# Split decays for the triangular sums, an earlier split of the gate factor, and no context modulation in the last layer

## The chip, the cores and the metric

The kernel runs on 1 core of one Trainium2 chip. The metric is the device time of one execution, in microseconds (us). A profiled execution gives its span (from the first to the last instruction on the core) and the trace from which all rows below are read.

## The reference

Two layers of a backbone work on 256 latent tokens and 256 context tokens of width 1024. Each layer has a modulated RMS norm, one input projection, three token mixers side by side (differential attention, chunked gated linear attention "GLA", neighbourhood attention), a gated merge with an output projection, then a second modulated norm and a squared-ReLU MLP. All is float32. What matters here:

```python
# modulation: six vectors of 1024 per layer, for the latent stream and for the context stream
mod = jax.nn.silu(c) @ w_mod[l] + b_mod[l]
mod_c = jax.nn.silu(c_ctx) @ w_mod[l] + b_mod[l]
sh1, sc1, g1, sh2, sc2, g2 = split(mod, 6);  sh1c, sc1c, g1c, sh2c, sc2c, g2c = split(mod_c, 6)
# the log decays of GLA, for the forward and the backward direction
z = ga[..., i * 16:(i + 1) * 16] @ a2[i] + ab[i]
log_a = log_sigmoid(z) / 16
cum = jnp.cumsum(log_a, within chunks of 64)
qe = q * exp(cum);  ke = k * exp(-cum);  kd = k * exp(cum_last - cum)
# the last layer returns the latent stream alone: there the context stream needs sh1c and sc1c only
if need_ctx:
    ctx = ctx + g1c * m_ctx
    ctx = ctx + g2c * sqrelu_mlp(rms_norm(ctx, norm2_g[l]) * (1.0 + sc2c) + sh2c, w_ff1[l], w_ff2[l])
```

## The kernel before

**Matrix products.** A product of two float32 operands is one matmul call, which the compiler turns into two matrix instructions (names as `pss<-la,tri` in the trace). Most products avoid it: both operands are split into a rounded half of type float32r ("high") and the remainder ("low"), and three calls (high by high, high by low, low by high) of one instruction each replace it. `split` does this for a tile: `copy` rounds it on ScalarE or VectorE (`act_first` picks the one that the planner expects to be done first), and VectorE subtracts. Weights come as pieces of 128x1024: a DMA on SP's queue into one of five `raw` buffers, a ScalarE copy (`wh<-raw`), a VectorE subtraction (`wl<-raw,wh`); `take()` hands the next piece to a product.

**Order.** Nothing is scheduled by the compiler: `drive` runs generators ("tasks") that emit instructions, and each engine, and each DMA queue, executes its instructions in the order in which they were emitted. A task yields a function that returns when its next step can start. `drive` takes the first task (in a fixed list: norms, attention, modulation, and last the stream of weight products) whose time has come by the planner's clock of TensorE, or else the one that comes first, and moves that clock there. The clock and the readiness of tiles come from constants of the kernel: a DMA takes `DMA_PER_BYTE` (2.9 us per MiB) after the last one, plus `LATENCY["DMA"]` = 2.0 us; an instruction takes `FIXED` + elements x `PER`. These constants decide the order only.

Two rules of lateness matter. A weight piece is split ahead of its use only while the planned ScalarE and VectorE are no further ahead of TensorE than `SPLIT_LATE` says, by how many pieces ahead it is:

```python
SPLIT_LATE = (INF, 1.5, 0.5, 0.0, 0.0, 0.0)     # us, index: pieces ahead of the one in use
if max(now["ACT"], now["DVE"]) > now["PE"] + SPLIT_LATE[min(n - st["cur"], 5)]: return False
```

A modulation product (`mods_task`; VectorE multiplies a 128x512 weight tile `wm` by the broadcast vector `cb` and sums along the row, once for the latent vector into `dump`, once for the context vector in place) is let in while VectorE is planned at most 1.0 us ahead of TensorE.

**The GLA gate.** The job `ga` starts behind the q/k products (`qk`) and ahead of the v products (`gv`). It issues three DMAs on SP's queue (`sb`, and the two `gl` tiles `ab` and `a2`), takes its weight piece, runs 24 matmuls (`psg<-h,wh` and `psg<-h,wl`, 512 columns), and splits their result into `gat`; then it splits the factor `a2` into `a2s`, which the trace calls `a`. `gla` waits for both, then multiplies (`pss<-a,gat`, 4 matmuls) and makes the log decays `la` on VectorE and ScalarE, and `tile_steps` sums them with the triangular matrices `tri` (`pss<-la,tri`) and with `ind`. While `gla` waits, the stream goes on with `gv`.

**Neighbourhood attention** of the first layer starts (in `branches`) when the last modulation group of that layer is done.

Of the kernel before, what the change touches and what calls it, by code (L numbers as in the profile page):

```python
# [151 lines left out]
def build(nc, tc, ctx, a):  # L152
# [18 lines left out]
    def const(name, shape, dtype=F32):  # L171
        return cpool.tile(shape, dtype, name=name, tag=name)
# [25 lines left out]
    def need(*aps, ps=None, n=1, lane=None, late=1.0):  # L198

        def f():  # L200
            t = pl.ready(aps)
            if ps:
                tag = ps if ps in PS else "s"
                i = n - 1 - (PS[tag] - len(ring.get(tag, ())))
                if i >= 0:
                    t = max(t, pl.touched(ring[tag][i]))
            if lane:
                t = max(t, now[lane] - late)
            return t
        return f  # L210
# [167 lines left out]
    ones = const("ones", [P, P])  # L378
    V.memset(ones, 1.0)
    rope = const("rope", [P, 2, 2, HD])  # L380
    tri = const("tri", [P, 4, P])
    ind = const("ind", [P, P])
    msk = const("msk", [P, 2, 4, P], U8)
    cc = const("cc", [P, KT, 2])
# [5 lines left out]
    scl = [[const(f"scl{l}{n}", [P, KT, 2]) for n in range(2)] for l in range(DEPTH)]  # L390


    def mod_scale(l, n, k0, k1):

        s = scl[l][n][:, k0:k1]
        g = sa[l][:, (SA_N1 if n == 0 else SA_N2) + k0:][:, 0:k1 - k0].unsqueeze(2).to_broadcast([P, k1 - k0, 2])
        V.scalar_tensor_tensor(s, mod[l][1 + 3 * n][:, k0:k1], 1.0, g, ADD, MULT)

    def mods_task():

        for l in range(DEPTH):
            yield after("consts" if l == 0 else MOD1_AFTER)

            groups = ((2, 4, 3, 5), range(6))[l]
            acc = {g: small("macc", [P, 2, KT, 2], 6) for g in groups}
            for ih in ((0,), (1,)) if l == 0 else ((0, 1),):
                cb = {}
                th = {}
                for i in ih:
                    for s in range(2):  # L410
                        cb[i, s], th[i, s] = u("cb"), u("cbt")
                        S.dma_start(cb[i, s], a["cr"][s, i].partition_broadcast(P))
                yield need(*cb.values(), lane="ACT")
                for k, c in cb.items():
                    S.activation(th[k], c, AF.Tanh, scale=0.5)
                    V.tensor_scalar(th[k], th[k], 0.5, 0.5, MULT, ADD)
                    G.tensor_tensor(c, c, th[k], MULT)
                todo = [(g, k, i) for g in groups for k in range(KT) for i in ih]
                loaded = []

                def load():
                    if todo:
                        g, k, i = todo.pop(0)
                        loaded.append((g, k, i, buf("wm", "wm", 512, NWM)))
                        MQ.dma_start(loaded[-1][3], a["w_mod"][l, g * KT + k, i])

                for _ in range(NWM):
                    load()
                while loaded:
                    g, k, i, w = loaded.pop(0)  # L430
                    for s in range(2):
                        yield need(w, cb[i, s], lane="DVE", late=MOD_LATE[l])
                        V.scalar_tensor_tensor(u("dump") if s == 0 else w, w, 1.0, cb[i, s], MULT, MULT,
                                               accum_out=acc[g][:, i, k, s:s + 1])
                    load()
                    if k == KT - 1 and i == 1:
                        yield need(acc[g], lane="DVE")
                        m = mod[l][g]
                        V.tensor_tensor(m, acc[g][:, 0], acc[g][:, 1], ADD)
                        b = sa[l][:, SA_BMOD + g * KT:SA_BMOD + (g + 1) * KT].unsqueeze(2).to_broadcast([P, KT, 2])  # L440
                        V.tensor_tensor(m, m, b, ADD)
                        if g in (1, 4):
                            mod_scale(l, g // 4, 0, KT)
                        done.add(("mod", l, g))


# [474 lines left out]
    def gla(L, y):  # L921
# [15 lines left out]
        yield need(*lt, lane="ACT")  # L937
        for t in (2, 3, 0, 1):
            S.activation(lt[t], lt[t], AF.Ln, bias=1.0)
        for t in (2, 3, 0, 1):  # L940
            V.scalar_tensor_tensor(la[t], la[t], 0.0, lt[t], ALU.min, SUB)

        yield after((l, "gv"))
        am0 = [u("amask") for _ in range(2)]
# [7 lines left out]
        for stage in range(2):  # L952
            tl = (2, 3) if stage == 0 else (0, 1)
            outs = stage == 1 or need_ctx
            qeT, at, ds, dec = [None] * 2, [None] * 2, [None] * 2, [None] * 2

            def tile_steps(b, t):
                lat = la[t]
                yield need(lat, ps="s")
                pr = psum("s")  # L960
                for r in range(2):
                    mm(hrd(pr)[:, :, r], tri[:, 2 + r, :], hrd(lat)[:, :, r], True, True)
                kd = u("kd")
                S.activation(kd, pr, AF.Exp)
                V.tensor_tensor(hrd(kd), hrd(kd), bc(qk[t][:, 256:512]), MULT)
                yield need(lat, ps="t")
                pd = psum("t")
                for h in range(4):
                    mm(pd[:, h * P:(h + 1) * P], lat[:, h * P:(h + 1) * P], ind, True, True)
                dc = small("dec", [P, 4, 2], 4)  # L970
                S.activation(dc, pd.rearrange("p (h c r) -> p h c r", h=4, c=2)[:, :, :, 0], AF.Exp)
                dec[b] = dc
                if outs:
                    yield need(lat, ps="s")
                    pc = psum("s")
                    for r in range(2):
                        mm(hrd(pc)[:, :, r], tri[:, r, :], hrd(lat)[:, :, r], True, True)
                    qe = u("qe")
                    S.activation(qe, pc, AF.Exp)
                    ke = u("ke")  # L980
                    S.activation(ke, pc, AF.Exp, scale=-1.0)
                    V.tensor_tensor(hrd(qe), hrd(qe), bc(qk[t][:, 0:256]), MULT)
                    V.tensor_tensor(hrd(ke), hrd(ke), bc(qk[t][:, 256:512]), MULT)
                ds[b] = []
                yield need(kd, ps="s", n=2)
                px = [psum("s"), psum("s")]
                for h in range(4):
                    for c in range(2):
                        rows = slice(64 * c, 64 * c + 64)
                        PE.matmul(px[c][:, h * P:(h + 1) * P], kd[rows, h * P:(h + 1) * P],  # L990
                                  v[t][rows, h * P:(h + 1) * P], start=True, stop=True, tile_position=(64 * c, 0))
                for c in range(2):
                    ds[b].append(u("ds"))
                    copy(ds[b][c], px[c])
                if not outs:
                    return
                yield need(ke, ps="t")
                keT = u("keT")
                copy(keT, transpose_4(ke))
                yield need(qe, ps="t")  # L1000
                qT = u("qeT")
                copy(qT, transpose_4(qe), HD ** -0.5)
                qeT[b] = qT
                yield need(keT, qT, ps="s", n=2)
                px = [psum("s"), psum("s")]
                for h in range(4):
                    for r in range(2):
                        rows = slice(64 * r, 64 * r + 64)
                        PE.matmul(px[r][:, h * P:(h + 1) * P], keT[rows, h * P:(h + 1) * P],
                                  qT[rows, h * P:(h + 1) * P], start=True, stop=True, tile_position=(64 * r, 0))  # L1010
                for r in range(2):
                    V.copy_predicated(am0[r], msk[:, r].rearrange("p h c -> p (h c)"), px[r])
                am = u("am")
                V.tensor_tensor(am, am0[0], am0[1], ADD)
                at[b] = am
# [50 lines left out]
    def start(l, h):  # L1066
# [25 lines left out]
        def ga():  # L1092
# [5 lines left out]

            a2s = u("a2", dtype=F32R)[0:96]
            L["gl"] = ab, a2s  # L1100
            yield piece
            w = take()
            yield need(*w, ps="g")
# [5 lines left out]
            gat = u("gat", dtype=F32R)[0:96]  # L1109
            copy(gat, ps[0:96])  # L1110
            V.tensor_tensor(gat[32:64], ps[32:64], gat[32:64].bitcast(F32), SUB)
            copy(a2s, a2[0:96])
            V.tensor_tensor(a2s[64:96], a2[64:96], a2s[64:96].bitcast(F32), SUB)
            L["gat"] = gat

        jobs.append(((l, "ga"), None, ga))
# [380 lines left out]
    def first_norm():  # L1497
# [13 lines left out]
            return after(("m01", k))()  # L1511

        yield from norm_apply(0, 0, x0, pb, 0, NTOK, NTOK, h, [0, 1], ready)
        for dst, n in ((tri, "tri"), (ind, "ind"), (rope, "rope")):
            S.dma_start(dst, a[n])
        mskf = u("mskf")[:, :2 * P].rearrange("p (r c) -> p r c", r=2)
        S.dma_start(mskf, a["msk"].rearrange("p (r c) -> p r c", r=2))
        for r in range(2):
# [136 lines left out]
```

## Time and profile before

| | |
|---|---|
| median of 3 runs | 1530.45 us (1530.14 to 1531.07) |
| the profiled execution | 1532.37 us, span 1530.3 us |
| mean granted TensorE clock | 0.998 of full |
| TensorE matmul busy (PE) | 1501.4 us, 98% of the span |
| VectorE busy (DVE) | 1105.0 us, 72% |
| ScalarE busy (ACT) | 705.2 us, 46% |
| GpSimd busy (POOL) | 22.5 us, 1% |
| DMA moved | 216.66 MB |

All instructions carry the line of one helper (L133), so rows are told apart by tile names, written `out<-in`. Matmuls are pipelined: the duration shown is longer than the time that one adds, which is the distance between starts. An entry in brackets at the end of a timeline row is the idle time of the engine before it and what ended it. SPq is SP's queue of DMA issues.

### The profile page before, as it was taken

To read this page: it belongs to the slowest core of one execution; us is meant where nothing else is said; L and a number is where in the kernel's file an instruction comes from. 1 tells how busy PE (TensorE), PEld (TensorE's weight loads), DVE (VectorE), ACT (ScalarE), POOL (GpSimd) and SP (SyncE) were. 2 spreads that over 40 slices of the span, in tenths; PEclk is the share of its full clock that TensorE was granted. 3 is DMA by queue.
4 is the path that set the end of the run, shared out by engine and by line. 5 is a ranking of instruction groups with operands and counts; after the bars stand their busy time and mean duration, and the time that the engine had idled before them with its cause. 6 is when DMAs were issued, how large, how long until landed. Compare 5 with 4: busy or idle time off the path is not lost.

```text
span 1530.3 us, 24161 instructions
## 1 busy us (share of the span) xinstructions
PE 1501.4 (98%) x9340; PEld 1281.9 (84%) x9340; DVE 1105.0 (72%) x2360; ACT 705.2 (46%) x1236; POOL 22.5 (1%) x30
## 2 busy tenths in 40 slices
PE   7999999999999899999999999999999999999999
PEld 5788878888887788888888888788888899899999
DVE  5687886687996676697786957777876766785543
ACT  4543535543235533723324153454465565477632
POOL 0100000000000100100000000000000000000000
PEclk9999999999999999999999999999999999999999
DMA  9531321157642232365564743322224325345662
GB/s 355 198 111 63 113 81 56 56 165 227 216 135 80 87 103 91 130 199 181 174 202 150 228 139 125 118 82 97 97 83 138 131 91 186 132 162 197 206 202 75
DMA packets 77794, 216.66 MB, mean 142 GB/s; under 512 B 9073, under 2 KB 12529, under 8 KB 77681
## 3 DMA queue, kind: packets, MB, share of 16 engines
q1 hardware_dynamic: 74880, 210.28, 42.3%
q10 hardware_dynamic: 2160, 2.76, 0.6%
q0 software_dynamic: 640, 2.10, 0.4%
q8 instruction: 73, 1.20, 0.3%
q14 instruction: 41, 0.33, 0.1%
HBM read 214.05 MB, written 1.05 MB: 141 GB/s over the span
## 4 chain that ended last, share of the span: by engine, by line
PE 89%; DVE 6%; ACT 2%; DMA 2%; issue 1%; SPq 0%; ACTq 0%; DVEq 0%
PE psg L133 77%; PE pss L133 12%; DVE wl L133 1%; ACT wh L133 1%; DMA wm<-w_mod 1%; DVE hn L133 1%; DMA gl<-gl 1%; DVE h L133 1%; DVE x L133 0%; DVE nt L133 0%; DMA sa<-sa 0%; ACT e L133 0%; SPq L133 0%; DVE nr L133 0%; ACT h L133 0%
## 5 line engine op out<-in xcount | busy, mean ns | idle before, releaser
L133 DVE TENSOR_TENSOR wl<-raw,wh 128x1024 fp32r<-128x1024 f32 x290 | 353.3, 1228 | 143.2 <-ACT wh L133 142.6
L133 PE MATMUL psg<-h,wh 128*128 128x256 f32 (+1 forms) x1808 | 447.3, 338 | 1.7 <-ACT wh L133 0.7
L133 ACT ACTIVATE wh<-raw 128x1024 fp32r<-128x1024 f32 x290 | 300.4, 1052 | 179.2 <-PE psg L133 166.4
L133 PEld LDWEIGHTS psg<-h,wh 128*128 128x128 f32 x1808 | 305.7, 189 | 42.3 <-issue 6.2
L133 PE MATMUL psg<-wh,h 128*128 128x512 f32 (+1 forms) x1056 | 338.8, 395 | 0.8 <-ACT h L133 0.8
L133 PE MATMUL psg<-h,wl 128*128 128x256 f32 (+1 forms) x904 | 302.8, 335 | 0.8 <-DVE wl L133 0.8
L133 PE MATMUL psg<-act,wh 128*128 128x256 f32 (+1 forms) x1056 | 250.8, 330 | 0.0
L133 PEld LDWEIGHTS psg<-wh,h 128*128 128x128 f32 x1056 | 197.2, 188 | 48.9 <-issue 2.1
L133 PE MATMUL psg<-wl,h 128*128 128x512 f32 (+1 forms) x528 | 206.7, 392 | 0.0
L133 PEld LDWEIGHTS psg<-act,wh 128*128 128x128 f32 x1056 | 178.2, 188 | 19.1
L133 PEld LDWEIGHTS psg<-h,wl 128*128 128x128 f32 x904 | 170.9, 189 | 19.5 <-DVE wl L133 1.2
L133 PE MATMUL psg<-act,wl 128*128 128x256 f32 (+1 forms) x528 | 174.4, 330 | 0.0
L133 DVE SCALAR_TENSOR_TENSOR dump<-wm,cb 128x512 f32<-128x512 f32 x160 | 109.7, 686 | 10.8 <-DMA wm<-w_mod 10.6
L133 PEld LDWEIGHTS psg<-wl,h 128*128 128x128 f32 x528 | 99.3, 188 | 21.3
L133 DVE SCALAR_TENSOR_TENSOR wm<-wm,cb 128x512 f32<-128x512 f32 x160 | 110.3, 689 | 4.0
L133 PEld LDWEIGHTS psg<-act,wl 128*128 128x128 f32 x528 | 99.2, 188 | 10.6
L133 PE MATMUL psg<-y,wh 128*128 128x512 f32 (+1 forms) x384 | 95.8, 339 | 0.0
L133 DVE TENSOR_TENSOR act<-r,act 128x256 fp32r<-128x256 f32 (+1 forms) x65 | 35.1, 540 | 72.8 <-ACT act L133 72.8
L133 ACT ACTIVATE r<-psg 128x256 f32<-128x256 f32 (+1 forms) x63 | 30.0, 476 | 107.5 <-PE psg L133 107.3
L133 PEld LDWEIGHTS psg<-y,wh 128*128 128x128 f32 x384 | 64.7, 188 | 8.8 <-issue 1.1
L133 PE MATMUL psg<-sp,wh 128*128 128x256 f32 (+1 forms) x304 | 65.3, 311 | 1.8 <-ACT sp L133 1.4
L133 PE MATMUL psg<-y,wl 128*128 128x512 f32 (+1 forms) x192 | 64.6, 337 | 0.0
(220 smaller groups left out, 1654.1 us busy)
## 6 DMA issues: line engine op xcount, KB each, us to landing
raw<-w_ff SPq DMA_DIRECT2D x128, 512.0 KB, 4.3
wm<-w_mod SPq DMA_DIRECT2D x192, 256.0 KB, 3.8
raw<-w_tok SPq DMA_DIRECT2D x72, 512.0 KB, 3.9
raw<-w_gate SPq DMA_DIRECT2D x48, 512.0 KB, 4.0
raw<-w_br SPq DMA_DIRECT2D x24, 512.0 KB, 3.6
raw<-w_out SPq DMA_DIRECT2D x16, 512.0 KB, 3.9
tb<-natb SPq DMA_DIRECT2D x16, 192.0 KB, 3.9
x<-xc SPq DMA_DIRECT2D x8, 256.0 KB, 4.5
```

Source lines behind the costliest of these rows:

```text
L133: r = f(*args, **kw)
```

## The change

Three edits. (1) In `gla`, each of the four decay tiles `la[t]` is split into two float32r halves, and each triangular sum (`sums`) becomes two float32r calls with the matrix `tri`, which is now float32r (its values are exact there; it is loaded through a float32 tile `trif` and copied by VectorE, after `ind` and `rope` on ScalarE's DMA queue). (2) In `ga`, the split of `a2` moves ahead of the job's weight piece and products, behind a wait for `a2`. (3) In the last layer, modulation groups 2 to 5 are computed for the latent vector alone.

```diff
--- before.py
+++ after.py
@@ -378,7 +378,7 @@
     ones = const("ones", [P, P])
     V.memset(ones, 1.0)
     rope = const("rope", [P, 2, 2, HD])
-    tri = const("tri", [P, 4, P])
+    tri = const("tri", [P, 4, P], F32R)
     ind = const("ind", [P, P])
     msk = const("msk", [P, 2, 4, P], U8)
     cc = const("cc", [P, KT, 2])
@@ -390,11 +390,11 @@
     scl = [[const(f"scl{l}{n}", [P, KT, 2]) for n in range(2)] for l in range(DEPTH)]
 
 
-    def mod_scale(l, n, k0, k1):
-
-        s = scl[l][n][:, k0:k1]
-        g = sa[l][:, (SA_N1 if n == 0 else SA_N2) + k0:][:, 0:k1 - k0].unsqueeze(2).to_broadcast([P, k1 - k0, 2])
-        V.scalar_tensor_tensor(s, mod[l][1 + 3 * n][:, k0:k1], 1.0, g, ADD, MULT)
+    def mod_scale(l, n, k0, k1, ns=2):
+
+        s = scl[l][n][:, k0:k1, :ns]
+        g = sa[l][:, (SA_N1 if n == 0 else SA_N2) + k0:][:, 0:k1 - k0].unsqueeze(2).to_broadcast([P, k1 - k0, ns])
+        V.scalar_tensor_tensor(s, mod[l][1 + 3 * n][:, k0:k1, :ns], 1.0, g, ADD, MULT)
 
     def mods_task():
 
@@ -429,18 +429,21 @@
                 while loaded:
                     g, k, i, w = loaded.pop(0)
                     for s in range(2):
+                        if l == DEPTH - 1 and s == 1 and g > 1:
+                            continue
                         yield need(w, cb[i, s], lane="DVE", late=MOD_LATE[l])
                         V.scalar_tensor_tensor(u("dump") if s == 0 else w, w, 1.0, cb[i, s], MULT, MULT,
                                                accum_out=acc[g][:, i, k, s:s + 1])
                     load()
                     if k == KT - 1 and i == 1:
                         yield need(acc[g], lane="DVE")
-                        m = mod[l][g]
-                        V.tensor_tensor(m, acc[g][:, 0], acc[g][:, 1], ADD)
-                        b = sa[l][:, SA_BMOD + g * KT:SA_BMOD + (g + 1) * KT].unsqueeze(2).to_broadcast([P, KT, 2])
+                        ns = 1 if l == DEPTH - 1 and g > 1 else 2
+                        m = mod[l][g][:, :, :ns]
+                        V.tensor_tensor(m, acc[g][:, 0, :, :ns], acc[g][:, 1, :, :ns], ADD)
+                        b = sa[l][:, SA_BMOD + g * KT:SA_BMOD + (g + 1) * KT].unsqueeze(2).to_broadcast([P, KT, ns])
                         V.tensor_tensor(m, m, b, ADD)
                         if g in (1, 4):
-                            mod_scale(l, g // 4, 0, KT)
+                            mod_scale(l, g // 4, 0, KT, ns)
                         done.add(("mod", l, g))
 
 
@@ -937,8 +940,11 @@
         yield need(*lt, lane="ACT")
         for t in (2, 3, 0, 1):
             S.activation(lt[t], lt[t], AF.Ln, bias=1.0)
+        las = [None] * 4
         for t in (2, 3, 0, 1):
             V.scalar_tensor_tensor(la[t], la[t], 0.0, lt[t], ALU.min, SUB)
+        for t in (2, 3, 0, 1):
+            las[t] = split(la[t])
 
         yield after((l, "gv"))
         am0 = [u("amask") for _ in range(2)]
@@ -954,12 +960,18 @@
             outs = stage == 1 or need_ctx
             qeT, at, ds, dec = [None] * 2, [None] * 2, [None] * 2, [None] * 2
 
+            def sums(i, t):
+
+                ps = psum("s")
+                for r in range(2):
+                    for j, x in enumerate(las[t]):
+                        mm(hrd(ps)[:, :, r], tri[:, i + r, :], hrd(x)[:, :, r], j == 0, j == 1)
+                return ps
+
             def tile_steps(b, t):
                 lat = la[t]
-                yield need(lat, ps="s")
-                pr = psum("s")
-                for r in range(2):
-                    mm(hrd(pr)[:, :, r], tri[:, 2 + r, :], hrd(lat)[:, :, r], True, True)
+                yield need(*las[t], ps="s")
+                pr = sums(2, t)
                 kd = u("kd")
                 S.activation(kd, pr, AF.Exp)
                 V.tensor_tensor(hrd(kd), hrd(kd), bc(qk[t][:, 256:512]), MULT)
@@ -971,10 +983,8 @@
                 S.activation(dc, pd.rearrange("p (h c r) -> p h c r", h=4, c=2)[:, :, :, 0], AF.Exp)
                 dec[b] = dc
                 if outs:
-                    yield need(lat, ps="s")
-                    pc = psum("s")
-                    for r in range(2):
-                        mm(hrd(pc)[:, :, r], tri[:, r, :], hrd(lat)[:, :, r], True, True)
+                    yield need(*las[t], ps="s")
+                    pc = sums(0, t)
                     qe = u("qe")
                     S.activation(qe, pc, AF.Exp)
                     ke = u("ke")
@@ -1098,6 +1108,9 @@
 
             a2s = u("a2", dtype=F32R)[0:96]
             L["gl"] = ab, a2s
+            yield need(a2)
+            copy(a2s, a2[0:96])
+            V.tensor_tensor(a2s[64:96], a2[64:96], a2s[64:96].bitcast(F32), SUB)
             yield piece
             w = take()
             yield need(*w, ps="g")
@@ -1109,8 +1122,6 @@
             gat = u("gat", dtype=F32R)[0:96]
             copy(gat, ps[0:96])
             V.tensor_tensor(gat[32:64], ps[32:64], gat[32:64].bitcast(F32), SUB)
-            copy(a2s, a2[0:96])
-            V.tensor_tensor(a2s[64:96], a2[64:96], a2s[64:96].bitcast(F32), SUB)
             L["gat"] = gat
 
         jobs.append(((l, "ga"), None, ga))
@@ -1511,8 +1522,11 @@
             return after(("m01", k))()
 
         yield from norm_apply(0, 0, x0, pb, 0, NTOK, NTOK, h, [0, 1], ready)
-        for dst, n in ((tri, "tri"), (ind, "ind"), (rope, "rope")):
+        for dst, n in ((ind, "ind"), (rope, "rope")):
             S.dma_start(dst, a[n])
+        trif = u("trif").rearrange("p (r c) -> p r c", r=4)
+        S.dma_start(trif, a["tri"])
+        V.tensor_copy(tri, trif)
         mskf = u("mskf")[:, :2 * P].rearrange("p (r c) -> p r c", r=2)
         S.dma_start(mskf, a["msk"].rearrange("p (r c) -> p r c", r=2))
         for r in range(2):
```

## Rows read from the trace of the kernel before

**Rows 1.** Page: busy time, share of the span, instructions

```profile
PE 1501.4 (98%) x9340; PEld 1281.9 (84%) x9340; DVE 1105.0 (72%) x2360; ACT 705.2 (46%) x1236; POOL 22.5 (1%) x30
```

**Rows 2.** Busy time by stretches: stretch, length, engines, clock, DMA share, GB/s

```profile
840.00:870.00 30.00, 30.00 (x133) 24.62 (x132) 29.55 (x78) 5.75 (x6) 0.00 (x0) 1.00 0.76 226
```

**Rows 3.** Groups by shape: count, then busy us, mean ns, idle before

```profile
L133 DVE SCALAR_TENSOR_TENSOR dump<-wm,cb 128x512 f32<-128x512 f32 x160 | 109.7, 686 | 10.8 <-DMA wm<-w_mod 10.6
L133 DVE DVE_READ_ACCUMULATOR wm<-wm,cb 128x1 f32 x160 | 13.1, 82 | 0.0
L133 DVE TENSOR_TENSOR sp<-m,sp 128x512 fp32r<-128x512 f32 x12 | 8.3, 692 | 8.5 <-ACT sp L133 8.5
L133 DVE TENSOR_TENSOR wl<-raw,wh 128x1024 fp32r<-128x1024 f32 x290 | 353.3, 1228 | 143.2 <-ACT wh L133 142.6 <-DMA wm<-w_mod 0.3
```

**Rows 4.** Tile tri; timeline of PE from 82 us; the chain's last row

```profile
L133 PE MATMUL pss<-la,tri x56: 377/379/454, 82.2 to 1032.5; 128*128 128x256 f32 x56
...
82.18 1.02 PE L133 MATMUL pss<-la,tri 128*128 128x256 f32 x4
83.04 1.05 PE L133 MATMUL pss<-ind,la 128*128 128x128 f32 x8
...
1353.65 173.37 PE psg L133 x1454
```

**Rows 5.** Timeline of the first layer's gate (SP, PE, ACT, DVE)

```profile
53.58 0.86 SPq L133 DMA_DIRECT2D gl<-gl  x2
57.26 0.39 PE L133 MATMUL psg<-wh,h 128*128 128x512 f32 x1
60.14 0.63 ACT L133 ACTIVATE a<-gl 96x512 fp32r<-96x512 f32 x1 [2.08 <-DMA gl<-gl]
60.80 0.68 DVE L133 TENSOR_TENSOR a<-gl,a 32x512 fp32r<-32x512 f32 x1 [2.02 <-ACT a L133]
61.54 1.20 PE L133 MATMUL pss<-a,gat 96*128 96x512 f32 x4 [1.31 <-DVE a L133]
63.04 0.69 DVE L133 SCALAR_TENSOR_TENSOR dump<-wm,cb 128x512 f32<-128x512 f32 x1 [1.38 <-DMA wm<-w_mod]
```

**Rows 6.** Timeline of the last layer's gate

```profile
982.58 2.94 ACT L133 ACTIVATE wh<-raw 128x1024 fp32r<-128x1024 f32 x3
984.00 0.90 SPq L133 DMA_DIRECT2D gl<-gl  x2
987.60 0.39 PE L133 MATMUL psg<-wh,h 128*128 128x512 f32 x1
990.64 0.63 ACT L133 ACTIVATE a<-gl 96x512 fp32r<-96x512 f32 x1 [2.25 <-DMA gl<-gl]
992.04 1.20 PE L133 MATMUL pss<-a,gat 96*128 96x512 f32 x4 [1.49 <-DVE a L133]
```

**Rows 7.** Landing times: tiles gl and wm; issues from 972 to 996 us

```profile
DMA to landing us min/median/max: 5.4/6.0/6.1
...
DMA to landing us min/median/max: 2.5/3.8/7.7
...
sb<-sb SPq DMA_DIRECT2D x1, 258.0 KB, 4.1
```

**Rows 8.** Timeline of DVE: the log decays of the first layer

```profile
73.58 2.50 DVE L133 SCALAR_TENSOR_TENSOR la<-la,lt 128x512 f32<-128x512 f32 x4 [0.72 <-ACT lt L133]
```

**Rows 9.** Timeline of DVE: last modulation group, then neighbourhood attention

```profile
435.38 0.17 DVE L133 TENSOR_TENSOR mod<-mod,sa 128x16 f32<-128x16 f32 x1
435.47 0.15 DVE L133 TENSOR_TENSOR nag<-sb 128x1 f32<-128x1 f32 x1
```

**Rows 10.** Busy time by stretches around a thin one, columns as in rows 2

```profile
600.00:604.00 4.00, 2.29 (x19) 2.08 (x18) 3.25 (x9) 2.44 (x6) 0.00 (x0) 1.00 0.25 92
604.00:608.00 4.00, 2.53 (x13) 2.15 (x12) 3.03 (x7) 1.78 (x2) 0.00 (x0) 0.78 0.21 60
608.00:612.00 4.00, 4.00 (x30) 4.00 (x30) 3.75 (x14) 1.46 (x3) 0.00 (x0) 0.79 0.63 206
```

## The prediction

> **What bounds the kernel now.** I read the busy times first: TensorE's matmuls fill 98% of the span [rows 1], so a change is worth what it takes from TensorE's own work or from the few waits of TensorE, and nothing else. Then the stretches: where the last layer's modulation runs, TensorE is busy 30.00 of 30 us while VectorE is at 29.55 [rows 2]; a full VectorE there holds nobody up. Third, the tile tri for the work that the change touches [rows 4]. Last, the timeline around the two places where the gate factor is split, for what is emitted on which queue, in which order [rows 5, 6]. There the reader is to see one pattern: the factor's tile lands some 6 us after its issue [rows 7], ScalarE sits idle until then, and TensorE waits 1.31 us and 1.49 us for it.
>
> **Triangular sums.** The 56 instructions [rows 4] are 28 float32 calls of 256 columns, two instructions each: 32 in the first layer (four tiles, two sums, two directions), 24 in the last (the context tiles lack the second sum). Four of them take 83.04 - 82.18 = 0.86 us, 0.215 us each. After the change there are again 56 instructions, but float32r ones. The trace has no such product with this strided operand. The nearest row is the float32r weight product of 256 columns: 173.37 us / 1454 = 0.119 us. Ends: 0.215 (no cheaper) and 0.107 (half). I take 0.119: same type, same columns. Gain 56 x 0.096 = 5.4 us: 3.1 in the first layer, 2.3 in the last, all on TensorE, which bounds here. Ends 0 and 6.0.
>
> **Splitting the decays.** Eight times a copy of 0.63 us (as the one of the factor [rows 5]) and a subtraction of 0.69 us [rows 3], four per layer. They come behind the last la, which ends at 73.58 + 2.50 = 76.08 us [rows 8]; four subtractions of 0.69 end near 78.9, and the first sum starts at 82.18 [rows 4], behind the v products. So they are covered by 3 us of v products; without that cover each layer would pay up to 3.5 us (0.63 + 4 x 0.69 + a start) once. They also push modulation products of the first layer back by 4 x 0.69 = 2.8 us of VectorE, and those end at 435.5 us, directly ahead of the first step of neighbourhood attention [rows 9], which is a real gate. I take 0, as the next edit brings more modulation products forward than that (below); end +2.8. The copy of tri costs VectorE at most 0.7 us [rows 3] some 30 us before the first sum: 0.
>
> **Last layer's modulation.** 4 groups x 8 x 2 = 64 context products of 0.686 + 0.082 us [rows 3] go: 49 us of VectorE. All of it lies where TensorE is full [rows 2], so I take 0. The weight tiles are still loaded, and each buffer comes free sooner, so the same DMAs bunch; the DMA share is 0.76 there already [rows 2]. Weight pieces stand five deep, about 5 x 24 x 0.226 = 27 us of products (0.226 is 30 us by 133 [rows 2]). A gain is excluded by the full TensorE, and a loss by those 27 us against the slowest landing of 7.7 us [rows 7].
>
> **The factor's split ahead of the products.** This is the edit that decides. It moves two instructions, but into the head of two queues that execute in order: whatever is emitted behind them on ScalarE and VectorE now waits for the landing, where before the weight splits and gat had gone first. What is behind them follows from the planner's constants. The three DMAs are planned at 3 x 0.73 + 2.0 = 4.2 us, so at r = start + 4.2 the split of a2 is emitted; it plans VectorE to r + 1.3. Only then does the job take its piece, which lets the next weight piece be split (allowed ahead 1.5): VectorE at r + 2.8. The 24 products take TensorE's clock to r + 5.2, and gat comes after them.
>
> *First layer.* Between r and gat VectorE is let up to 1.0 us ahead of TensorE, in steps of 0.60 from r + 2.8: five modulation products. So VectorE's queue reads: a, wl, five products, gat. The DMA issue does not move (53.58), so a starts at 60.14 and 60.80 as now [rows 5]; ScalarE's wh of about 1 us [rows 6] ends near 61.8, wl of 1.2 us [rows 3] at 63.0, five products of 0.77 at 66.8, gat at 67.5. The tiles of those products land around 63.0 [rows 5], in time. TensorE meanwhile does what is emitted before pss<-a,gat: the 24 products (their own piece was split earlier, so they run as now), then nine v products instead of twelve, as the planner no longer counts the factor's split behind gat. From 57.26 [rows 5] at 0.23 us each they end at 59.3. So pss<-a,gat starts at 67.55 instead of 61.54 with three products fewer done: 6.0 + 0.7 = **+6.7 us**. Ends: +2.9 (no modulation products ahead of gat: gat at 63.7) and +8 (they wait for their tiles).
>
> *Last layer.* No modulation is left. The last copy of the q/k products puts ScalarE 0.25 + 0.31 = 0.56 us ahead in the plan, just over the 0.5 allowed two pieces ahead, so the first v piece is not split before a, and this time the v products themselves wait. Today three pieces are split from 982.58 on [rows 6], under the gate's products; afterwards they stand behind a. If a starts at 990.64 as now, the first wl ends at 993.45, three of them at 995.8, gat at 996.45: pss<-a,gat at 996.5 instead of 992.04, three products fewer: +5.2. The three weight DMAs now sharing the queues would be gone; if the tile then lands in 4.1 us as sb did [rows 7] instead of 6.1, it is +3.2. I take the middle, **+4.2**.
>
> *The clock.* In the first layer TensorE would stand still from 59.3 to 67.5. After the thin stretch 600 to 606 (2.29 of 4 us busy, then single products) the granted clock averages 0.78 and 0.79 over 8 us, a part of it at 1.2 GHz: (0.22 + 0.21) x 4 = 1.7 us of work lost [rows 10]. I add 1.6 for the first layer, and nothing for the last, where products lie between the waits; ends 0 and 3.4.
>
> **A rule against this.** The landing of 6.0 us carries the forecast [rows 7]. The Trainium skill (DMA: Bandwidth & Descriptors, "Anatomy of one DMA — SWDGE (gpsimd) path") fits a transfer as about 2.0 us plus its bytes at 436 GB/s, for GpSimd's path; by that 256 KB would take an estimated 2.6 us. The trace disagrees here, with 5.4 to 6.1 us behind other transfers; what an early landing would do is rival A below.
>
> **Sum.** -5.4 + 6.7 + 4.2 + 1.6 = +7.1 us, on the profiled span of 1530.3 us (0.46%). That execution took 1532.37 us, 1.9 above the median of 1530.45; the difference is carried to the median: **1537.5 us**.
>
> **Rivals.** (A) *The stall is small and the sums pay for it.* For: a tile of 256 KB can land in 2.5 us [rows 7]; for a: a starts at 56.9. Then wl ends at 59.7, five products at 63.5, gat at 64.2: +3.4; in the last layer a starts at 987.4, gat ends at 993.2: +1.9. With -5.4: about 1530. Against: all four gl transfers took 5.4 us or more, under a loaded queue. (B) *Faster.* The weight splits, the modulation products and gat are emitted ahead of a after all, or TensorE finds other work at that place. Then the sums' 5.4 us remain, and up to 2.8 us of today's two waits go: 1522 to 1525, say 1524.5. It decides if the two delays of pss<-a,gat together stay under 5.4 us. For: neither wait is in the trace of before, their size hangs on an order that I worked out by hand. Against: attention has nothing else to give TensorE there, it waits for this job. (C) *The sums get no cheaper,* because a strided operand streams in float32r as slowly as now: 1543. Against: four blocks of 64 columns are read in both cases, and nothing in the rows makes the stride the limit.
>
> **How the numbers follow.** Forecast 0.60, A 0.15, B 0.15, C 0.10. The forecast's own range: the gate from +2.9 + 3.2 to +8 + 5.2, clock 0 to 3.4, sums -6.0 to -4, with not all ends at once: 1533 to 1544. With A at its upper part and C inside, the range is 1528.5 to 1544.5; it leaves out B and single extremes. A measurement of this kernel tells about 0.2%, 3.1 us: faster is below 1527.4, slower above 1533.5. Slower holds the forecast, C and a little of A, less the forecast's low edge: 0.70; same 0.14, faster 0.16.
>
> **What the profile after would show.** Right: 56 pss<-la,tri instructions, 0.12 us apart; 96 context products (wm<-wm,cb) instead of 160, with TensorE as full as now in that stretch; a<-gl ahead of wh on ScalarE, which idles 5 us or more before it; pss<-a,gat with 5 to 8 us of TensorE idle in the first layer; in the last a wait of the first v product for wh; a clock under 1.0 behind the first wait. Wrong: a<-gl found behind the splits or gat, a landing under 3 us, or la,tri still 0.215 us apart. The whole would also be wrong if the first layer's neighbourhood attention started by as much earlier or later as its modulation ends [rows 9].

## The result and the profile after

The changed kernel takes 1545.42 us (median, 1544.75 to 1545.87) against 1530.76 us of the kernel before on the same chip: ratio 1.0102, 95% interval 1.0084 to 1.0120 (the two medians alone give 1.0096), slower by 14.7 us. The forecast was 1537.5 us, its range ended at 1544.5.

TensorE does as much as before [rows 1], in a span of 1543.3 us instead of 1530.3; the time in which it does nothing grew from 28.9 to 42.2 us. So all that was lost is idle time of TensorE, or busy time at a lower clock with other work saved. Busy times on the page after:

```profile
PE 1501.1 (97%) x9340; PEld 1280.6 (83%) x9340; DVE 1069.7 (69%) x2241; ACT 709.1 (46%) x1244; POOL 21.1 (1%) x30
```

**The first layer's gate.** Timeline of SP, ACT, DVE and PE after, to be held against [rows 5]:

```profile
53.61 0.86 SPq L133 DMA_DIRECT2D gl<-gl  x2
58.87 0.63 ACT L133 ACTIVATE a<-gl 96x512 fp32r<-96x512 f32 x1 [5.01 <-DMA gl<-gl]
60.48 1.23 DVE L133 TENSOR_TENSOR wl<-raw,wh 128x1024 fp32r<-128x1024 f32 x1 [0.26 <-DMA wm<-w_mod]
61.62 0.68 DVE L133 SCALAR_TENSOR_TENSOR dump<-wm,cb 128x512 f32<-128x512 f32 x1
...
64.39 0.69 DVE L133 SCALAR_TENSOR_TENSOR dump<-wm,cb 128x512 f32<-128x512 f32 x1
65.12 0.68 DVE L133 TENSOR_TENSOR gat<-psg,gat 32x512 fp32r<-32x512 f32 x1
65.86 1.65 PE L133 MATMUL pss<-a,gat 96*128 96x512 f32 x3 [6.43 <-DVE gat L133]
```

VectorE's queue reads a, wl, five modulation products, gat, as forecast. TensorE, which waited 1.31 us for the factor, now waits 6.43 us for gat. The factor landed faster than in the profile before ([rows 7]: 6.0 us). Landing times of the tile gl after:

```profile
DMA to landing us min/median/max: 4.6/4.7/4.8
```

**The last layer's gate**, against [rows 6]:

```profile
994.33 0.63 ACT L133 ACTIVATE a<-gl 96x512 fp32r<-96x512 f32 x1 [6.05 <-DMA gl<-gl]
995.94 3.50 DVE L133 TENSOR_TENSOR wl<-raw,wh 128x1024 fp32r<-128x1024 f32 x3 [0.26 <-ACT wh L133]
999.47 0.68 DVE L133 TENSOR_TENSOR gat<-psg,gat 32x512 fp32r<-32x512 f32 x1
1000.21 2.07 PE L133 MATMUL pss<-a,gat 96*128 96x512 f32 x4 [4.76 <-DVE gat L133]
```

Three weight splits that ran at 982.58 under the gate's products [rows 6] stand behind the factor, and gat behind them.

**The clock** fell within both waits, while TensorE stood still, and was still low behind them. Windows of 2 us after (length, busy PE, PEld, DVE, ACT, POOL, granted clock, DMA share, GB/s):

```profile
64.00:66.00 2.00, 0.14 (x1) 0.14 (x1) 1.94 (x7) 0.00 (x0) 0.00 (x0) 0.50 0.84 261
66.00:68.00 2.00, 2.00 (x5) 1.63 (x6) 1.94 (x3) 0.00 (x0) 0.00 (x0) 0.50 0.29 99
68.00:70.00 2.00, 2.00 (x6) 1.54 (x6) 1.97 (x4) 0.70 (x2) 0.00 (x0) 0.50 0.76 244
70.00:72.00 2.00, 2.00 (x9) 1.64 (x8) 1.93 (x4) 1.19 (x2) 0.00 (x0) 0.85 0.05 18
...
998.00:1000.00 2.00, 0.00 (x0) 0.00 (x0) 1.97 (x3) 1.23 (x2) 0.00 (x0) 0.76 0.81 248
1000.00:1002.00 2.00, 1.79 (x4) 1.49 (x5) 1.94 (x4) 0.00 (x0) 0.00 (x0) 0.50 0.84 277
1002.00:1004.00 2.00, 2.00 (x6) 1.53 (x5) 1.93 (x4) 0.63 (x1) 0.00 (x0) 0.50 0.87 289
1004.00:1006.00 2.00, 2.00 (x6) 1.54 (x6) 1.97 (x4) 1.02 (x2) 0.00 (x0) 0.54 0.59 236
```

Before, the stretches behind pss<-a,gat show 1.00:

```profile
63.00:65.00 2.00, 2.00 (x10) 1.59 (x10) 1.81 (x5) 0.00 (x0) 0.00 (x0) 1.00 0.59 237
...
994.00:996.00 2.00, 2.00 (x10) 1.61 (x9) 1.93 (x4) 0.63 (x1) 0.00 (x0) 1.00 0.59 199
```

0.50 is the 1.2 GHz level. Busy time times what is missing of the clock: 0.5 x 2 + 0.5 x 2 + 0.15 x 2 = 2.3 us in the first layer, 0.5 x 1.79 + 0.5 x 2 + 0.46 x 2 = 2.8 us in the last.

**The sums.** Timeline of PE and ACT after, against [rows 4]:

```profile
89.33 0.62 PE L133 MATMUL pss<-sp,tri 128*128 128x256 f32 x4
90.14 1.28 ACT L133 ACT_TABLE_LOAD   x1
90.60 1.20 PE L133 MATMUL pss<-sp,tri 128*128 128x256 f32 x8
91.43 0.60 ACT L133 ACTIVATE kd<-pss 128x512 f32<-128x512 f32 x1
92.09 1.16 PE L133 MATMUL pss<-ind,la 128*128 128x128 f32 x8 [0.29 <-ACT kd L133]
```

Eight of them in the last layer stand between 1040.06 and 1041.09 us, 0.129 us each on average (one step of 0.20, the others of about 0.12). The saving is 56 x (0.216 - 0.129) = 4.9 us of TensorE. But the last row shown waits: the exponentials that free the PSUM buffers could not start before ScalarE's table load ended at 91.42.

**The rest.** The splits of the decays ran under v products, as forecast (VectorE, 78.57 us; the sums start at 89.33). 96 context products instead of 160 [rows 3]; the first layer's modulation ends 4.9 us later than before, and neighbourhood attention directly behind it [rows 9]. TensorE's products start 5.9 to 6.0 us later than before on both sides of that place (380 to 520 us), so the later modulation costs nothing more there:

```profile
78.57 2.49 DVE L133 TENSOR_TENSOR sp<-la,sp 128x512 fp32r<-128x512 f32 x4
...
440.25 0.18 DVE L133 TENSOR_TENSOR mod<-mod,sa 128x16 f32<-128x16 f32 x1
440.34 0.15 DVE L133 TENSOR_TENSOR nag<-sb 128x1 f32<-128x1 f32 x1
```

### The profile page after: what moved, and what is told of

Read it like the earlier page. It is cut to its first block, busy times and chain, and to the rows that moved or that the text cites. A ratio compares the mean times of both kernels' runs of the same rounds, so it can differ in the third digit from the quotient of the medians.

```text
span 1543.3 us, 24027 instructions
## 1 busy us (share of the span) xinstructions
PE 1501.1 (97%) x9340; PEld 1280.6 (83%) x9340; DVE 1069.7 (69%) x2241; ACT 709.1 (46%) x1244; POOL 21.1 (1%) x30
## 4 chain that ended last, share of the span: by engine, by line
PE 88%; DVE 6%; ACT 2%; DMA 2%; issue 1%; SPq 0%; ACTq 0%; DVEq 0%
PE psg L133 77%; PE pss L133 11%; DVE wl L133 1%; DMA wm<-w_mod 1%; DVE hn L133 1%; DVE h L133 1%; ACT wh L133 1%; DVE nt L133 0%; SPq L133 0%; DMA gl<-gl 0%; DVE x L133 0%; DMA sa<-sa 0%; ACT h L133 0%; DVE y L133 0%; DVE nr L133 0%
## 5 line engine op out<-in xcount | busy, mean ns | idle before, releaser
L133 DVE SCALAR_TENSOR_TENSOR x<-psg,mod,x 128x256 f32<-128x256 f32 x96 | 43.1, 480 | 48.2 <-PE psg L133 47.7
L133 DVE SCALAR_TENSOR_TENSOR wm<-wm,cb 128x512 f32<-128x512 f32 x96 | 66.2, 690 | 2.6
```

Source lines behind the costliest of these rows:

```text
L133: r = f(*args, **kw)
```

## The experiments

Each was timed beside the kernel before on the same chip (1530.85, 1530.72 and 1530.90 us for the three groups of four; these and the 1530.76 above lie within 0.2 us, so times are compared across the groups). Theory 1: the gate's move alone makes the loss, and the sums give back only a part of what they save. Its rivals stand in each expectation.

### One part at a time

**gate_alone**: the kernel before with edit (2) alone (the place from which the two instructions go is cut here).

```diff
+            yield need(a2)
+            copy(a2s, a2[0:96])
+            V.tensor_tensor(a2s[64:96], a2[64:96], a2s[64:96].bitcast(F32), SUB)
             yield piece
```

> Only the gate factor's split is moved ahead of the products. Theory 1 (the gate pays all of the loss, the cheaper sums and the dropped modulation give nothing): the two delays of pss<-a,gat (5.0 and 3.2 us, three products included) and two stretches at half clock (2.1 and 2.2 us) return alone: about 12.5 us slower than the kernel before, 1543 us. Rival 2 (the sums do give their 5 us, and the dropped modulation or the reordering costs as much): here too up to 12.5 us, but then sums_alone and mods_alone differ from the kernel before by 4 us or more, with opposite signs. Rival 3 (the loss is mostly the interplay of the edits): under 9 us slower here.

Measured 1546.39 us, ratio 1.0103 (1.0088 to 1.0118): +15.5 us. PE rows of the two waits:

```profile
67.13 2.07 PE L133 MATMUL pss<-a,gat 96*128 96x512 f32 x4 [7.60 <-DVE gat L133]
...
1002.64 1.98 PE L133 MATMUL pss<-a,gat 96*128 96x512 f32 x4 [4.74 <-DVE gat L133]
```

The move alone makes the whole loss. In the first layer of this profile the factor landed as late as in the profile before (ScalarE starts a at 60.14 us in both), and pss<-a,gat starts at 67.13 us, where the prediction had 67.55.

**sums_alone**: edit (1) alone (split decays, float32r sums).

> Only the decays' split and the float32r sums. Theory 1: the 56 instructions are 0.13 us apart instead of 0.216, but the time goes to waits around them: within 1.5 us of the kernel before, 1529 to 1532 us. Rival 2: 4.5 to 5.5 us faster, 1525 to 1526 us. Rival 3: anything between.

Measured 1528.94 us, ratio 0.9984 (0.9975 to 0.9992): 1.9 us less, where 4.9 us of TensorE's work went.

**mods_alone**: edit (3) alone.

> Only the last layer's context modulation left out (groups 2 to 5 of the last layer have no context column). Theory 1: TensorE is full in that stretch, within 1 us of the kernel before. Rival 2: 4 us or more slower, through the order of the last layer's instructions or the weight loads that bunch. Rival 3: within 2 us.

Measured 1530.12 us, ratio 0.9993 (0.9984 to 1.0001): nothing that can be told from no change.

**no_gate**: the changed kernel with the gate's split back behind its products, (1) and (3) kept.

> The changed kernel with the gate factor's split back behind the products; sums and modulation as changed. Theory 1: 1529 to 1532 us, as the kernel before. Rival 2: the same, as sum of -5 and +5. Rival 3: clearly faster, about 1525 us, since the interplay is gone.

Measured 1528.53 us, ratio 0.9985 (0.9976 to 0.9993). Against the changed kernel it is 16.9 us faster. The same instructions of TensorE start 8.7 us later in the changed kernel from 80 to 320 us, 9.6 us just ahead of the last layer's gate and 17.2 us from 1000 to 1350 us: about half of the price in each layer, and nearly all of it the gap plus the low clock (6.43 + 2.3 = 8.7 us and 4.76 + 2.8 = 7.6 us).

### What in the gate's move costs

**after_early**: the split ahead of the products as changed, but the two gl loads are issued some 5 us earlier in the first layer (ScalarE's queue, behind the constants) and ahead of the q/k job in the last (the step that loads them is cut here).

```diff
-            ab, a2 = u("gl"), u("gl")
-            for i, t in enumerate((ab, a2)):
-                SP.dma_start(t, a["gl"][l, i])
+            ab, a2 = GL[l]          # loaded by an earlier step
```

> The changed kernel with the two gl loads issued earlier: in the first layer on ScalarE's DMA queue behind the constants, in the last layer on SP's queue one job sooner, ahead of the q/k products. Order of the split in front of the products as in the changed kernel. Theory (the loss is the wait for the landing at the head of ScalarE's and VectorE's queues, and the clock that falls behind it): a starts without idle time before it, the two gaps ahead of pss<-a,gat shrink from 6.4 and 4.8 us to under 1 us, no stretch at half clock, 1523 to 1529 us. Rival (the order itself costs: weight splits and modulation products ahead of gat, landing or not): 2 to 4 us of each gap stay, 1533 to 1540 us.

Measured 1529.19 us, ratio 0.9992 (0.9983 to 1.0000). VectorE starts the factor without idle time (tile a):

```profile
55.03 0.41 DVE L133 CAST a<-gl 96x512 fp32r<-96x512 f32 x1
57.33 4.09 DVE L133 TENSOR_TENSOR wl<-raw,wh 128x1024 fp32r<-128x1024 f32 x2 [0.38 <-ACT wh L133]
61.46 0.68 DVE L133 TENSOR_TENSOR gat<-psg,gat 32x512 fp32r<-32x512 f32 x1
...
980.10 0.42 DVE L133 CAST a<-gl 96x512 fp32r<-96x512 f32 x1
981.27 3.50 DVE L133 TENSOR_TENSOR wl<-raw,wh 128x1024 fp32r<-128x1024 f32 x3
985.96 0.68 DVE L133 TENSOR_TENSOR gat<-psg,gat 32x512 fp32r<-32x512 f32 x1 [1.20 <-ACT gat L133]
```

No gap of 0.25 us or more stands ahead of pss<-a,gat, and the clock stays at 1.00 behind it. In the last layer VectorE's queue reads a, three weight splits, gat, as in the changed kernel: with the landing out of the way that order costs nothing. In the first layer the order is not the same: the planner, for which the tile has landed, lets in no modulation product ahead of gat. So this run does not tell the landing there from what is let in; the next two do. The time is at the upper end of what was expected; this profile is 2.3 us behind that of the kernel before from its first products on, ahead of anything that was edited.

**after_pool**: the two instructions that split the factor on GpSimd.

```diff
-            copy(a2s, a2[0:96])
-            V.tensor_tensor(a2s[64:96], a2[64:96], a2s[64:96].bitcast(F32), SUB)
+            G.tensor_copy(a2s, a2[0:96])
+            G.tensor_tensor(a2s[64:96], a2[64:96], a2s[64:96].bitcast(F32), SUB)
```

> The changed kernel with the two instructions that split the factor put on GpSimd, which is idle 99% of the time; the loads are issued where they were. Theory (what costs is what stands behind the waiting instruction on ScalarE and VectorE): nothing stands behind it on GpSimd, weight splits and gat run under the products as before the change, TensorE waits 1.5 to 3.5 us for GpSimd ahead of pss<-a,gat in each layer, no or a short half clock, 1527 to 1533 us. Rival (the landing itself comes too late for the place, whoever waits for it): gaps of 4 to 6 us as now, 1540 to 1546 us.

Measured 1536.74 us, ratio 1.0038 (1.0025 to 1.0050), between the two. Its timeline:

```profile
60.22 1.75 POOL L133 TENSOR_TENSOR a<-gl,a 32x512 fp32r<-32x512 f32 x1
60.97 1.55 DVE L133 SCALAR_TENSOR_TENSOR wm<-wm,cb 128x512 f32<-128x512 f32 x1
...
65.86 0.68 DVE L133 TENSOR_TENSOR gat<-psg,gat 32x512 fp32r<-32x512 f32 x1
...
66.69 2.04 PE L133 MATMUL pss<-a,gat 96*128 96x512 f32 x4 [6.79 <-DVE gat L133]
...
994.75 1.19 PE L133 MATMUL pss<-a,gat 96*128 96x512 f32 x4 [1.92 <-POOL a L133]
```

In the last layer the theory holds: nothing stands behind the wait, the gap is 1.92 us. In the first it failed: the factor is ready at 61.97, yet gat comes at 65.86, behind seven modulation products. The planner's wait for a2 lets them in ahead of gat, whichever engine splits the factor. So there is a second share beside the landing. A part of this delay is the run's own: VectorE's instructions were slowed beside GpSimd (1.55 us in the second row; see the last section).

**after_noyield**: the changed kernel without the line `yield need(a2)`.

> The changed kernel without the line that lets the job wait for a2 by the planner's clock: the split of the factor is emitted at once behind the loads, so the landing is still waited for at the head of ScalarE's and VectorE's queues, but between it and gat neither weight splits nor modulation products are let in (VectorE: a, two cbt, gat). Theory (two shares: the landing, some 1.5 to 2.5 us in each layer, and what the planner lets in between the factor and gat, some 4 us in the first layer and 3.5 us in the last, with the clock that falls behind): gaps of 2 to 3 us, 1532 to 1538 us. Rival (the landing is all of it): gaps of 5 us or more in both layers as in the changed kernel, 1542 to 1546 us.

Measured 1537.26 us, ratio 1.0034 (1.0024 to 1.0044). In the first layer VectorE now has only two cbt between a and gat (in the last, one weight split instead of three):

```profile
60.01 0.63 ACT L133 ACTIVATE a<-gl 96x512 fp32r<-96x512 f32 x1 [6.65 <-DMA gl<-gl]
...
62.19 0.68 DVE L133 TENSOR_TENSOR gat<-psg,gat 32x512 fp32r<-32x512 f32 x1
```

The gaps of TensorE at these places are 2.97 and 2.73 us. Both shares are there: 8.2 us (1545.42 - 1537.26) for what is let in, with its low clock in the last layer, and 8.7 us (1537.26 - 1528.53) for the landing that is still waited for. By the profiles only 2.3 us of the first share lie in the first layer: the clock fell behind the gap of 2.97 us too (0.50 from 64 to 68 us), and stayed at 1.00 behind that of 2.73 us.

**after_fill**: the changed kernel with idle products that fill most of the two gaps.

```diff
+            if t == 0:
+                for _ in range(18 if l else 24):
+                    nc.tensor.matmul(ps, L["h"][0][0][:, 0:P], L["h"][0][0][:, 0:512], start=True, stop=True)
             mm(ps, gat[:, t * P:(t + 1) * P], a2, True, True)
```

> The changed kernel with 24 (first layer) and 18 (last layer) idle products of 512 columns ahead of the first pss<-a,gat, some 5.4 and 4.1 us of TensorE, which lie in the two gaps of 6.4 and 4.8 us. They delay nothing; their result is overwritten. Theory (some 4 us of the loss are the clock, which falls to half behind each gap): granted clock 1.00 in the 6 us behind each, gaps gone but gat as late as now, 1541 us. Rival (the delay is all, the low clock costs nothing since other waits follow): 1545 us as the changed kernel.

Measured 1541.60 us, ratio 1.0071 (1.0057 to 1.0085): 3.8 us less than the changed kernel, for some 9.6 us more work of TensorE (42 products of 0.23 us). The windows show why:

```profile
66.00:68.00 2.00, 1.36 (x6) 1.14 (x7) 1.94 (x4) 0.00 (x0) 0.00 (x0) 1.00 0.66 184
...
1000.00:1002.00 2.00, 2.00 (x10) 1.63 (x9) 1.94 (x3) 0.52 (x1) 0.00 (x0) 1.00 0.82 283
```

The clock's share is real, some 4 to 5 us in both layers together; a part of it is hidden here, as the factor happened to land later (ScalarE starts a at 59.65 us in the first layer, 0.8 us behind the changed kernel).

### Where the sums' saving goes

**sums_high**: sums_alone with the high half alone in each sum (28 instructions fewer; the low halves are left out).

> The kernel before with the split decays, but with the high half alone in each triangular sum (28 instructions instead of 56; the low halves are left out of the sums, so the decays are those of a rounded operand). Theory (around the sums ScalarE's exponentials and VectorE's evacuations, not TensorE, set when the next PSUM buffer is free, so TensorE's saving turns into waits): within 1 us of the kernel with the sums alone (1528.9), the waits next to the sums grow. Rival (the sums lie on TensorE's path and each instruction saved counts): 28 x 0.125 = 3.5 us less, 1525.4 us.

Measured 1532.06 us, ratio 1.0011 (1.0000 to 1.0021), outside both expectations: the planner's costs changed with the calls, and from some 220 us on it emitted TensorE's instructions in another order; its profile ends 3.4 us behind that of sums_alone. It tells nothing of the sums. The next two keep the order exactly, by telling the planner of the same two calls.

**sums_f32** and **sums_half**: sums_alone's order, with the float32 sum of before, or with the high half alone (the two real calls are shortened to one line here).

```diff
                     for j, x in enumerate(las[t]):
-                        mm(hrd(ps)[:, :, r], tri[:, i + r, :], hrd(x)[:, :, r], j == 0, j == 1)
+                        pl.note("PE", "matmul", (hrd(ps)[:, :, r], tri[:, i + r, :], hrd(x)[:, :, r]), {})
+                    nc.tensor.matmul(...)      # one call: float32 la[t], or the high half
```

> The kernel with the sums alone, in exactly its order of instructions, but with each triangular sum as one float32 call on the unsplit decays, as before the change; the splits are made all the same. So only the 56 instructions differ in length (0.216 against 0.129 us, 4.9 us of TensorE). Theory (about half of the 4.9 us is given back as waits for ScalarE and VectorE next to the sums): 2 to 3 us above the kernel with the sums alone (1528.9), 1531 to 1532 us, and the small waits next to the sums are gone. Rival 1 (all on TensorE's path): 1533.8 us. Rival 2 (the gain of the sums-alone kernel is another order or an earlier landing, not the sums): 1529 us.

> The kernel with the sums alone, in exactly its order, with the high half of the decays alone in each sum: 28 instructions fewer, 3.5 us of TensorE (the low halves are left out of the sums, so the decays are those of a rounded operand). The run with the high half before this one had another order in the modulation. Theory (what is saved next to the sums turns into waits): 0 to 1.5 us under the kernel with the sums alone, 1527.5 to 1529 us, the waits next to the sums grow by 2 us or more in all. Rival (on the path): 1525.4 us.

Measured 1531.61 us (ratio 1.0006, 0.9998 to 1.0015) and 1529.12 us (ratio 0.9985, 0.9976 to 0.9993), against 1528.94 for sums_alone. The first 4.9 us taken from TensorE gave 2.7 us (each of the two times is known to about 1.3 us, so something between 1 and 4.5), the next 3.5 us (an estimate, 28 x 0.125) gave nothing that can be measured. TensorE's waits from 80 to 135 us and from 1000 to 1080 us, in sums_f32:

```profile
PE pss L966 <- DVE y L133: 0.3, 1, 0.3
...
PE psg L133 <- ACT z L133: 1.8, 1, 1.8
```

in sums_alone:

```profile
PE pss L133 <- DVE y L133: 1.1, 2, 0.7
PE pss L133 <- ACT kd L133: 0.3, 1, 0.3
...
PE pss L133 <- DVE kd L133: 0.6, 1, 0.6
PE pss L133 <- ACT ke L133: 0.5, 1, 0.5
```

in sums_half:

```profile
PE pss L966 <- DVE y L133: 1.6, 2, 0.9
PE pss L133 <- ACT kd L133: 1.0, 1, 1.0
...
PE pss L133 <- DVE kd L133: 2.5, 2, 1.4
```

Waits for what VectorE and ScalarE do to PSUM next to the sums (pss rows): 0.3, then 2.5, then 5.1 us. The saving turns into them: 2.5 - 0.3 = 2.2 of the first 4.9 us, 2.6 of the next 3.5. The wait of 1.8 us for z stands in all three profiles and in the changed kernel's, with the float32 sum too, but not in the profile before: it belongs to the order that the splits bring, not to the sums.

### A version that beats both

**nogate_early**: no_gate with the early loads of after_early.

> A version that may beat both: sums and modulation as changed, the factor split behind the products as before the change, and the loads of the factor issued earlier. Theory (the wait for the landing, 1.3 and 1.5 us in the profile before, goes in both layers whatever the queue does): 1526 to 1528 us, no gap ahead of pss<-a,gat. Rival (these waits were gone already in the kernel without the gate's move, whose factor landed in 4.6 us): 1528.5 us as that kernel.

Measured 1528.17 us, ratio 0.9985 (0.9976 to 0.9993), the same as no_gate: in that kernel's profile TensorE had no wait for the factor left to remove. Either is 2.3 to 2.7 us faster than the kernel before, and 17 us faster than the changed one.

## Why the prediction was wrong in size and right in sign

**Right.** The gate's move decides, by the mechanism forecast: the landing is waited for at the head of ScalarE's and VectorE's queues, and weight splits, five modulation products and gat stand behind it. The instruction order of the first layer came out as written. Rival A fell: the tile landed in 4.7 us, between the rival's 2.5 and the forecast's 6.0, and the gaps were still 6.43 and 4.76 us. Rival B fell: the order was not another. Rival C fell as well: a strided sum takes 0.129 us, close to the 0.119 chosen. The modulation edit was worth 0 (1530.12 against 1530.85). The split decays were covered in place; sums_f32 puts the splits with the order that they bring at +0.7 us (interval -0.3 to +2.3), where the forecast had 0; the wait for z is in it. In gate_alone, where the factor landed as the forecast assumed, the first layer's delay is 67.13 - 61.54 + 0.7 = 6.3 us against the 6.7 forecast.

**The steps that failed:**

- *The clock: "I add 1.6 for the first layer, and nothing for the last, where products lie between the waits".* Both layers fell to 1.2 GHz: 2.3 and 2.8 us by the windows, 3.8 us by after_fill. In the last layer products did lie before the wait, but TensorE then stood still 4.76 us in one piece, and the clock fell within it. The price itself differs from one execution to the next: behind the thin stretch from which it was read [rows 10], the profile after shows 1.00 (604 to 620 us).
- *The sums: "all on TensorE, which bounds here", -5.4.* The work saved was 4.9 us, the time 2.7 us. TensorE is 98% busy on average, but around the sums the PSUM buffers come back at the pace of ScalarE's exponentials and VectorE's products, and that is the limit that sums_half met. The Trainium skill (ScalarE: Activation LUTs, "What ACT_TABLE_LOAD costs") puts a switch of tables at about 1.28 us for the load and 1.38 us for a drain. The trace agrees on the load (1.28 us at 90.14) and shows no further drain: the load starts 0.02 us behind ScalarE's last z, and kd starts at 91.43, 0.01 us behind the load.
- *The base: "the difference is carried to the median".* The profile before took 1.9 us more than its median, the profile after (1545.56) 0.1 us more. The two waits of 1.31 and 1.49 us that I set off against the new ones are part of such an execution: with the same order of instructions at this place, the sum of both was under 0.5 us in no_gate's profile, about 1.2 in mods_alone's and 0.7 in sums_alone's. They come from a late landing: 5.4 to 6.1 us in the profile before, where the eleven other profiles with the loads at this place have medians of 4.6 to 5.2 us. So the new waits replace less than I took off. That these waits make the 1.9 us is argued, not tried.
- *The gate's own delay, +6.7 and +4.2.* It was over-sized by 2.6 us against the profile before, which hid a part of the terms above: 65.86 - 61.54 + 0.7 = 5.0 us in the first layer, as the tile landed 1.3 us sooner, and 3.3 us in the last (lateness of pss<-a,gat 8.2 us against 5.6 us ahead of the gate, and three products). In the last layer the step also named the wrong wait: the first v piece had been split in time, v products ran until 995.45, and TensorE waited for gat itself.

By runs the change adds up as: gate +15.5 (gate_alone) to +16.9 (against no_gate), sums -2.7, splits and order +0.7, modulation -0.7; together +12.8 to +14.2, where 14.7 was measured. By the forecast's own terms: 7.1, plus 3.5 for the clock (5.1 against 1.6), plus 2.7 for the sums, less 2.6 for the gate's delay (8.3 against 10.9) is 10.7; the two profiled spans differ by 13.0, so some 2.3 us net lie in waits at other places, the one for z (1.8 us) above all; the last 1.7 us, from 13.0 to 14.7, are the base.

## What to carry to other kernels

An instruction that waits for a transfer costs what stands behind it on its in-order queue, and also what a planner lets in during the wait: ask for both, load earlier or leave it behind work that needs no transfer. A wait of several us that leaves TensorE wholly idle is to be priced with the slow clock behind it: here 5.1 us beside 11.2 us of waits. A stage is bounded by what returns its buffers, whatever the busy share of the span says; halve the suspected cost once more with the order held fixed, and see if the time follows.

## What the runs showed of the hardware that was not expected

The same product on VectorE took 0.69 us beside an idle GpSimd and 1.55 us while GpSimd subtracted (60.97 us in after_pool), and GpSimd's subtraction of 32x512 took 1.75 to 2.24 us where VectorE takes 0.68.

In the profile of after_noyield the last 150 us ran faster at the same granted clock: 178 products of 256 columns in 20 us, against 173 in the kernel before. That execution took 1531.46 us, 5.8 under its median; what set the pace was not found. Single executions 5 to 7 us under their median occur with the kernel before as well (1523.45 us at a median of 1530.72), but none of those was profiled. First after_noyield, then before:

```profile
1480.00:1500.00 20.00, 20.00 (x178) 20.00 (x178) 9.53 (x10) 8.30 (x8) 0.00 (x0) 1.00 0.64 209
```

```profile
1480.00:1500.00 20.00, 20.00 (x173) 20.00 (x172) 9.28 (x9) 7.42 (x7) 0.00 (x0) 1.00 0.62 201
```
